# Expert weights in consecutive rows per partition, with features and activations in the matching order

## The chip, the cores and the metric

One core of a Trainium2 chip runs the whole program. The metric is device time in microseconds from the first to the last work of one execution. The engines are named as the profile names them: PE is TensorE (PEld its weight loads), DVE is VectorE, ACT is ScalarE, POOL is GpSimd, and SP is the engine whose queue issues the weight transfers.

## The reference, cut to what matters

Two transformer blocks on 256 tokens of 1024 features, in float32. The first block ends in a mixture of 32 experts, four of them for each token. This is the part that the change touches:

```
def clamped_swiglu(hdn):
    x_glu = jnp.minimum(hdn[..., :D_EXPERT], SWIGLU_LIMIT)
    x_lin = jnp.clip(hdn[..., D_EXPERT:], -SWIGLU_LIMIT, SWIGLU_LIMIT)
    return x_glu * jax.nn.sigmoid(SWIGLU_ALPHA * x_glu) * (x_lin + 1)

def expert_block(args):
    xb, e = args
    hdn = xb @ w_gate_up[e] + b_gate_up[e]          # [rows, 1024] @ [1024, 2048]
    return clamped_swiglu(hdn) @ w_down[e] + b_down[e]   # [rows, 1024] @ [1024, 1024]
```

Both matrix products sum over 1024 rows of a weight matrix. The sum doesn't depend on the order of the rows, as long as the other operand lists its features in the same order.

## The kernel before

**Weights.** Each expert has 12 MB of weights: `w_gate_up` in four chunks of 256 rows, `w_down` in two chunks of 512 rows, 2 MB each. The function `fill` issues them on the SP queue (L208), in the order of `plan`, as soon as a tile of the ring is free; eight tiles of 128 partitions by 16 KB are in use in most of the stage, and a chunk's tile becomes free when `release` is reached after its last product. Before the change, partition p of a `gu` chunk holds rows p and 128 + p of the chunk (two runs of 8 KB), and partition p of a `dn` chunk holds rows p, 128 + p, 256 + p and 384 + p (four runs of 4 KB).

**Features.** `h2t` holds the normed tokens (tokens on partitions, 1024 features along the row). `gain_h2` (L959, POOL) multiplies by the gain, which `along` has spread over all partitions (L805, PE, and L813, ACT), and `h2_rows` (L969, DVE) adds the shift, also spread by `along`. Expert 0's features are gathered from `h2t` at L1068, those of the others by `gather` (L1114).

**One expert.** The loop runs over 32 experts. `gate_up` makes 64 products (L1157, two halves of 64 PE columns side by side) and starts its sums with the bias (L1147). Then DVE and ACT apply the activation: L1162 (minimum, from PSUM), L1164 (sigmoid, ACT), L1165 (product), and then for each half of 256 columns L1168 (clip, from PSUM into `lin`) and L1169 (plus one, times `sig`). PE transposes `lin` in four pieces (L1175), ACT copies the result to `aT` (L1179), and `down` makes 32 products (L1197). Behind each `gate_up` and each `down` stands a branch (L1419, L1462) for experts with more than 64 tokens; three experts take it here (9, 13 and 20, counted from 0), and `act_q` (L1269 to L1274) is the same activation for their further slots.

**Order between experts.** Two experts' outputs are summed into the tokens at once. So an expert with an even number from 4 on begins its activation while PE still has `combine2` (L1220, 16 products) of the pair before to do; an expert with an odd number has only two transposes there (`sgT`, L1127). Experts 0 to 2 also gather the next expert's features at this place (L1114).

Of the kernel before, what the change touches and what calls it, by code (L numbers as in the profile page):

```python
# [27 lines left out]
OP = mybir.AluOpType  # L28
# [11 lines left out]
# columns of the per-partition vectors (vecs)  # L40
# [11 lines left out]
def _consts():  # L52
# [15 lines left out]
    # rows of eight heads: sums' high and low parts and ones, on the queries' side and (negated) on the keys'  # L68
# [27 lines left out]
def build(tc, A, out, dbg=None):  # L96
# [51 lines left out]
    for e in range(NE):  # L148
        for j in range(4):
            add(("gu", e, j), A["w_gate_up"][e, 256 * j:256 * j + 256, :].rearrange("(k p) f -> p k f", p=128))  # L150
        for j in range(2):
            add(("dn", e, j), A["w_down"][e, 512 * j:512 * j + 512, :].rearrange("(k p) f -> p k f", p=128))
# [27 lines left out]
    def fill():  # L180
        while state["issued"] < len(plan):
# [6 lines left out]
            # the slot that has been free for the longest time  # L188
# [11 lines left out]
            if i == last_e + 3:  # L200
                # the last chunks before block 2 come in parts
                for f in (slice(0, 1024), slice(1024, 2048)):
                    nc.sync.dma_start(dst[:, :, f], src[:, :, f])
            elif i in (last_e + 4, last_e + 5):
                for k in (slice(0, 2), slice(2, 3), slice(3, 4)) if i > last_e + 4 else (slice(0, 2), slice(2, 4)):
                    nc.sync.dma_start(dst[:, k], src[:, k])
            elif i >= 6:
                nc.sync.dma_start(dst, src)  # L208
# [13 lines left out]
    def split(pool, src, shape, tag, bufs, pattern=None):  # L222
        """src (float32) = hi + lo, both of 12 significant bits"""
# [6 lines left out]
    class Stream:  # L230
        """pieces of weights, 512 columns each, split ahead of their products"""
# [33 lines left out]
    def cols(key, kk=KD, tiles_=4):  # L265
        """pieces of a column chunk: 128 columns, four rows of k-tiles each"""
# [7 lines left out]
    def krows(key, nk, n=512):  # L274
        """pieces of a chunk: 512 columns of one k-tile"""
        m = n // 512
        return [(key, lambda c, i=i: c[:, 512 * i:512 * i + 512], i == nk * m - 1) for i in range(nk * m)]
# [6 lines left out]
    def rstd_of(pool, ps_sum, n, eps, newton=None):  # L284
        """1/sqrt(ps_sum/n + eps), [128, T]; a step of Newton's where newton gives its scratch"""
# [16 lines left out]
    # ================= block 1: modulation, projections, attention =================  # L302
# [7 lines left out]
    # only for the first eight heads  # L310
# [27 lines left out]
    # the first chunks come in parts, in the order of their use  # L338
# [14 lines left out]
    # at column 5 of a stationary, zeros around it: 32 columns from 5 - r on give row r of the product  # L353
    nc.vector.tensor_copy(cs32[:, :, 5], sg)

    # silu(c) along the rows of all partitions
# [11 lines left out]
    # modulation: mod[n] = sum_d silu(c)[d] W[d, n] + b  # L368
# [3 lines left out]
    # of a chunk's features, DVE sums two tiles (their rows transposed), and PE the other two  # L372
# [9 lines left out]
    def ada_rows(j, r, tag="sc"):  # L382
        """row r of the next sums takes the products with chunk j"""
# [13 lines left out]
    def ada_sum(n, dst, b, row=None, tag="sc", bufs=2):  # L397
        """sums over the four groups of rows, features on partitions: dst and b are [128, 2, n]"""
# [7 lines left out]
    # sum of squares of x  # L406
# [30 lines left out]
    def first_products(n, k):  # L437
        """the four tiles of chunk n of w_in, the products of one k-tile"""
# [51 lines left out]
    def gain(name, sc0, g):  # L490
        """g * (1 + scale)"""
# [4 lines left out]
    # MoBA: the bias of a head is a function of q - k; row p has key k at column 127 - p + k of the table. The table goes  # L496
    # out 16 times, and comes back 16 rows at a time that start one element earlier each
# [21 lines left out]
    # projections  # L519
# [29 lines left out]
    # b_gate_up and b_down as exact sums of three bfloat16 parts  # L549
    bg = keep.tile([128, 3072], BF, name="bg")  # L550

    def expert_bias(i):
        """in three stages, for the columns of different calls"""
# [32 lines left out]
    # forget gates (four times, at rows 0..31): log_sigmoid, running sums  # L586
# [24 lines left out]
    def forget_b():  # L611
        """the sums as two parts of 12 bits each, so that a head's bias is one product of exact terms"""
# [26 lines left out]
    # attention  # L639
# [77 lines left out]
    # the other projections and the rest of the modulation run between the heads  # L717
# [50 lines left out]
    # out projection, tokens on partitions: its products with the heads that are through run between the later heads  # L768
# [4 lines left out]
    def out_products(n):  # L773
        """n of the 32 products, two to a piece of weights"""
# [25 lines left out]
    def along(dst, col, tag="sc", bufs=2, cs=(0, 1)):  # L800
        """a value per feature, along the rows of all partitions"""
        for c in cs:
            p = ps.tile([128, 512], F32, name=tag, bufs=bufs)
            for i in range(4):
                nc.tensor.matmul(p[:, 128 * i:128 * i + 128], lhsT=col[:, 4 * c + i:4 * c + i + 1].to_broadcast(  # L805
                    [128, 128]), rhs=ident, start=True, stop=True, skip_group_check=True)
# [8 lines left out]
    def logits_rows(t, tag, bufs):  # L815
        """what the router makes of xT's tokens t, four groups of rows to be summed"""
# [11 lines left out]
    for h in range(8, 17):  # L828
# [27 lines left out]
        if h == 14:  # L856
            # the part of the router's logits that comes from the shift
# [6 lines left out]
        if h == 15:  # L864
            xt = pa.tile([128, 2, D], F32, name="qkb")
            nc.scalar.dma_start(xt, A["x"])
            # and the part that comes from x before its own norm is known
# [14 lines left out]
    # the products are through: the room of their operands goes to the ring  # L882
# [6 lines left out]
    # the last chunks of the modulation, while the norms and the router wait  # L889
# [19 lines left out]
    def rstd1(dst, tt):  # L909
        """from the two halves' mean squares"""  # L910
# [11 lines left out]
    # post norm and residual, tokens on partitions: x1 = x + rstd * t. The router's logits take t as it is  # L922
# [12 lines left out]
    def turned(tt, src):  # L935
        """features on partitions"""
# [18 lines left out]

    def gain_h2(tt):
        for i in range(4):
            s = slice(256 * i, 256 * i + 256)
            nc.gpsimd.tensor_mul(h2t[:, tt, s], xt[:, tt, s], gfb[i])  # L959
# [31 lines left out]
    along(gfb, gain_["f"])  # L991
# [26 lines left out]
    along(shb, mod[:, 24:32])  # L1018
# [6 lines left out]
    # router  # L1025
# [22 lines left out]
    # slot of a token at an expert; far away where the expert isn't chosen  # L1048
# [15 lines left out]
    # the first expert's slots, at once with features on partitions  # L1064
# [10 lines left out]
    # ================= experts =================  # L1075
# [14 lines left out]
    def slots(e, r, pair=None, S=None):  # L1090
        """one-hot of 64 slots of the expert at its tokens, plain and times the gate: the first 64, or those from
        32 + 64 r on. The gated ones of two experts share a tile, a further round has its own twice"""
# [16 lines left out]
    def gather(S):  # L1109
        """rows of the slots: [(half of the features, slot), 512]"""  # L1110
# [9 lines left out]
    def gatherT(x, r=0):  # L1120
        """k-tile 4 h + c of the slots' features lies at [:, c, 64 h:]"""
# [15 lines left out]
    def gate_up(e, xe, r=0, hook=None):  # L1137
# [3 lines left out]
        for j in range(4):  # L1141
            w = None if r else chunk(("gu", e, j)).rearrange("p (k f) -> p k f", k=2)
            for i, p in enumerate((pg, pl_)):
# [5 lines left out]
                for kk in range(2):  # L1149
                    k = 2 * j + kk  # L1150
                    if r:
                        wk = again(A["w_gate_up"][e, 128 * k:128 * k + 128, 1024 * i:1024 * i + 1024])
# [14 lines left out]
        for c in (slice(0, 256), slice(256, 512)):  # L1167
            nc.vector.tensor_scalar(l[:, c], pl_[:, c], 7.0, -7.0, op0=OP.min, op1=OP.max)  # L1168
            nc.vector.scalar_tensor_tensor(l[:, c], l[:, c], 1.0, s[:, c], op0=OP.add, op1=OP.mult)  # L1169
        return l  # L1170

# [10 lines left out]
    def down(e, at, r=0):  # L1182
# [6 lines left out]
        for c in range(2):  # L1189
            w = None if r else chunk(("dn", e, c)).rearrange("p (k f) -> p k f", k=4)  # L1190
            for j in range(4):
                if r:
                    wk = again(A["w_down"][e, 512 * c + 128 * j:512 * c + 128 * j + 128, :])
# [10 lines left out]
        # two experts' rows on top of each other  # L1204
# [24 lines left out]
    # slots 64 .. 95: 32 slots in each column tile  # L1229
# [37 lines left out]
    def act_q(p, l):  # L1267
# [4 lines left out]
        nc.vector.tensor_scalar(l, p[64:128], 7.0, -7.0, op0=OP.min, op1=OP.max)  # L1272
        nc.vector.scalar_tensor_tensor(l, l, 1.0, g, op0=OP.add, op1=OP.mult)
        nc.vector.tensor_mul(l, l, s)  # L1274
# [25 lines left out]
    # position buckets of block 2 (both signs), then its bias table: a step at each expert  # L1300
# [53 lines left out]
    # pieces of the weights of block 2  # L1354
    def by_half(p):
        """four tiles of two pieces: first all the first halves"""
# [41 lines left out]
    for e in range(NE):  # L1398
        if e == 2:
            # the smallest ring is through: its room goes to what comes later  # L1400
# [3 lines left out]
        if e == NE - 1:  # L1404
            # the last rings are through: their room goes to the pieces of block 2
# [5 lines left out]
        # an expert with more than 64 tokens: 32 further slots  # L1411
# [14 lines left out]
        def hook(j):  # L1426
# [4 lines left out]
            # a chunk of the first experts makes room at once  # L1431
# [39 lines left out]
    # experts with more than 96 tokens: rounds of 64 slots, which load the weights again  # L1471
# [14 lines left out]
    # the last two experts' rows, post norm  # L1486
# [29 lines left out]
    # ================= block 2 =================  # L1516
# [4 lines left out]
    def begin(xh, xl, g, make_x, add, third):  # L1521
        """splits x * g and starts with four tiles of products, with the rest of the norm. make_x(k) completes a
        k-tile of x"""
# [5 lines left out]
        def products(k):  # L1529
# [5 lines left out]
            for t in range(4):  # L1535
                # a bank starts once, and the tile that comes second in it writes on the cleared flags
# [124 lines left out]
    def mixer(make_x):  # L1661
# [12 lines left out]
        # the second ring is through: its two tiles hold what the mixer keeps  # L1674
# [108 lines left out]
        # the attention's steps, then the Fourier branch's, between the tiles of the projections  # L1783
        k_tile2(0)
        # lambda
# [16 lines left out]
        # rstd with tokens on partitions  # L1802
# [60 lines left out]
    def out_proj(k):  # L1863
        # the products are two tiles ahead of the sums, which read banks that no product writes
# [144 lines left out]
```

## Time and profile before

| | us |
|---|---|
| median of 3 runs (1783.46 to 1786.46) | 1783.85 |
| span of the profiled execution | 1783.1 |
| expert stage in it (first L1157 to last L1197) | 214.8 to 1203 |

The profile's busy times are shares of the whole span; the expert stage is 55% of it and has its own limits, so the rows below are mostly of that stage. A timeline row gives the start, the duration, the engine and line, the tile written and the tiles read, the shapes and the count of instructions merged; in brackets stands the idle time of the engine before it and who ended that. The clock column (PEclk) is the granted TensorE clock as a share of 2.4 GHz; the chip grants either 1.2 or 2.4 GHz here, and a window with a value in between holds both.

### The profile page before, as it was taken

How to read it: one execution, taken by the hardware profiler on the slowest of the kernel's cores; microseconds unless marked ns; L12 is line 12 of the kernel's file. 1: busy time of each engine (PE TensorE's matmuls, PEld its weight loads, DVE VectorE, ACT ScalarE, POOL GpSimd, SP SyncE). 2: the span in 40 equal slices, each digit the busy share in tenths (PEclk: the TensorE clock that was granted, in tenths of full speed). 3: DMA queues.
4: the chain of work that ended last, by engine and by line, in shares of the span. 5: the costliest groups of instructions: out<-in, count | busy, mean ns of one | idle time of the engine just before them, and what ended most of it. 6: DMA issues, size and time to landing. Idle time of an engine off the chain costs nothing. (4 is left out here: it accounts for less than half of the span.)

```text
span 1783.1 us, 25545 instructions
## 1 busy us (share of the span) xinstructions
PE 1666.5 (93%) x10162; PEld 1061.4 (60%) x10162; DVE 780.9 (44%) x1627; ACT 525.8 (29%) x1113; POOL 91.3 (5%) x98
## 2 busy tenths in 40 slices
PE   6999999999989989999999999997999999999998
PEld 5787633333433333333333333336999989999997
DVE  5776613232432432324211111115766777676665
ACT  4544310111111011011111101114555555665444
POOL 3501100000000000000000000002000000310000
PEclk8999999999999999999999999998999999999999
DMA  9878799999989988999889999993544453344530
GB/s 353 329 221 332 281 372 410 385 415 418 414 352 380 415 329 361 416 416 415 355 364 415 418 414 417 415 415 145 189 172 184 189 207 142 142 150 182 214 142 25
DMA packets 89005, 548.81 MB, mean 308 GB/s; under 512 B 5064, under 2 KB 7912, under 8 KB 49448
## 3 DMA queue, kind: packets, MB, share of 16 engines
q1 hardware_dynamic: 88424, 544.55, 77.1%
q8 instruction: 115, 1.88, 0.4%
q0 software_dynamic: 272, 0.92, 0.2%
q10 hardware_dynamic: 144, 1.05, 0.2%
q14 instruction: 50, 0.41, 0.1%
HBM read 545.25 MB, written 1.25 MB: 306 GB/s over the span
## 5 line engine op out<-in xcount | busy, mean ns | idle before, releaser
L1157 PE MATMUL h<-ring,xe 128*64 128x512 f32 x2048 | 465.5, 593 | 5.6 <-ACT xe L1080 0.4
L251 DVE TENSOR_TENSOR wl<-ring,wh 128x512 fp32r<-128x512 f32 x421 | 285.1, 710 | 116.3 <-ACT wh L250 109.5
L1157 PEld LDWEIGHTS h<-ring,xe 128*64 128x64 f32 x2048 | 165.6, 136 | 250.5 <-issue 246.5
L250 ACT ACTIVATE wh<-ring 128x512 fp32r<-128x512 f32 x424 | 248.9, 622 | 107.6 <-PE gu L281 85.1
L1197 PE MATMUL h<-ring,aT 128*64 128x512 f32 x1024 | 234.8, 612 | 5.5 <-ACT aT L1179 5.5
L280 PE MATMUL gu<-ring,wh 128*128 128x256 f32 x704 | 201.2, 286 | 2.9 <-ACT ring L1541 2.9
L281 PE MATMUL gu<-ring,wh 128*128 128x256 f32 x704 | 200.4, 285 | 1.9 <-DVE ring L1545 1.9
L282 PE MATMUL gu<-ring,wl 128*128 128x256 f32 x704 | 200.4, 285 | 0.0
L1162 DVE TENSOR_SCALAR glu<-h 128x512 f32<-128x512 f32 x32 | 22.1, 692 | 370.8 <-PE h L1157 370.8
L1197 PEld LDWEIGHTS h<-ring,aT 128*64 128x64 f32 x1024 | 72.6, 141 | 148.7 <-issue 134.4
L1213 DVE COPY y<-h 64x512 f32<-64x512 f32 x32 | 22.2, 694 | 310.2 <-ACTq L1462 285.7
L280 PEld LDWEIGHTS gu<-ring,wh 128*128 128x128 f32 x704 | 135.9, 193 | 3.5 <-ACT ring L1541 3.3
L281 PEld LDWEIGHTS gu<-ring,wh 128*128 128x128 f32 x704 | 135.9, 193 | 2.2 <-DVE ring L1545 2.1
L282 PEld LDWEIGHTS gu<-ring,wl 128*128 128x128 f32 x704 | 135.9, 193 | 0.0
L1117 ACT ACTIVATE glu<-rot 128x512 f32<-128x512 f32 x31 | 18.5, 597 | 276.9 <-PE rot L1114 274.4
L280 PE MATMUL pd<-acth,wh 128*128 128x256 f32 x352 | 98.7, 280 | 0.1
L281 PE MATMUL pd<-actl,wh 128*128 128x256 f32 x352 | 98.3, 279 | 0.1
L282 PE MATMUL pd<-acth,wl 128*128 128x256 f32 x352 | 98.2, 279 | 0.0
L1212 ACT ACTIVATE y<-h 64x512 f32<-64x512 f32 x31 | 18.3, 590 | 220.7 <-PE h L1197 123.1
L1350 DVE COPY_PREDICATED bias<-bm,vecs 128x512 f32<-128x512 uint8 x124 | 80.1, 727 | 1.1
L280 PE MATMUL gu<-big_h,wh 128*128 128x256 f32 x256 | 74.6, 291 | 0.0
L282 PE MATMUL gu<-big_h,wl 128*128 128x256 f32 x256 | 71.5, 279 | 1.1 <-DVE wl L251 1.1
(422 smaller groups left out, 2287.1 us busy)
## 6 DMA issues: line engine op xcount, KB each, us to landing
ring<-in_w_gate_up SPq DMA_DIRECT2D x127, 2048.0 KB, 14.0
ring<-in_w_down SPq DMA_DIRECT2D x62, 2048.0 KB, 19.8
ring<-in_ffn_gu SPq DMA_DIRECT2D x22, 2048.0 KB, 7.8
ring<-in_win SPq DMA_DIRECT2D x12, 2048.0 KB, 8.5
ring<-in_ffn_wd SPq DMA_DIRECT2D x10, 2048.0 KB, 9.5
ring<-in_ada SPq DMA_DIRECT2D x8, 2048.0 KB, 11.1
ring<-in_wout SPq DMA_DIRECT2D x4, 2048.0 KB, 8.1
ring<-in_ada SPq DMA_DIRECT2D x4, 1024.0 KB, 12.6
```

What stands on the lines that cost most here:

```text
L250: nc.scalar.activation(dh, src, AF.Copy)
L251: (eng or nc.vector).tensor_tensor(dl, src, dh.bitcast(F32), op=OP.subtract)
L280: nc.tensor.matmul(o, lhsT=wh, rhs=mh, start=start, stop=False, skip_group_check=True)
L281: nc.tensor.matmul(o, lhsT=wh, rhs=ml, start=False, stop=False, skip_group_check=True)
L282: nc.tensor.matmul(o, lhsT=wl, rhs=mh, start=False, stop=stop, skip_group_check=True)
L1117: nc.scalar.activation(x, p, AF.Copy)
L1157: nc.tensor.matmul(p[64 * hf:64 * hf + 64], lhsT=x, rhs=wk[:, 512 * hf:512 * hf + 512], start=False, stop=(k == KD - 1), skip_group_check= ...
L1162: nc.vector.tensor_scalar(g, pg, 7.0, None, op0=OP.min)
L1197: nc.tensor.matmul(py[64 * oh_:64 * oh_ + 64], lhsT=at[:, j, 64 * c:64 * c + 64], rhs=wk[:, 512 * oh_:512 * oh_ + 512], start=False, stop= ...
L1212: nc.scalar.activation(pair["y"][o:o + 64, 0:512], py[0:64], AF.Copy)
L1213: nc.vector.tensor_copy(pair["y"][o:o + 64, 512:1024], py[64:128])
L1350: nc.vector.copy_predicated(bias2[:, h], m, val[:, :, None].to_broadcast([128, 2, T]))
```

## The change

A chunk is now read as consecutive rows: partition p of a `gu` chunk holds rows 2p and 2p + 1, and partition p of a `dn` chunk rows 4p to 4p + 3, in either case one run of 16 KB. So the tile numbered kk in a `gu` chunk holds the features 2p + kk, and the tile numbered j in a `dn` chunk the activations 4p + j. `h2t` is stored in that order: `along` writes the gain and the shift in the new order (PE writes PSUM in steps of 128 columns, two at a time), and `gain_h2` reads the tokens in natural order and writes them in the new one. The activation reads its PSUM sums and `sig` in steps of four columns (16 bytes) and writes `lin` in consecutive columns, so that the four transposes find their columns next to each other. The number of instructions and their order on every engine are as before; DVE's, POOL's and PE's named instructions have other access patterns. The last three chunks of the last expert still come in parts.

```
-            add(("gu", e, j), A["w_gate_up"][e, 256 * j:256 * j + 256, :].rearrange("(k p) f -> p k f", p=128))
+            add(("gu", e, j), A["w_gate_up"][e, 256 * j:256 * j + 256, :].rearrange("(p k) f -> p k f", p=128))
-            add(("dn", e, j), A["w_down"][e, 512 * j:512 * j + 512, :].rearrange("(k p) f -> p k f", p=128))
+            add(("dn", e, j), A["w_down"][e, 512 * j:512 * j + 512, :].rearrange("(p k) f -> p k f", p=128))
+            elif i >= 6 and key[0] in ("gu", "dn"):
+                nc.sync.dma_start(t[0:parts, 0:cols], src.rearrange("p k f -> p (k f)"))
...
+                o = p[:, 128 * i:128 * i + 128]
+                if sorted_:
+                    o = p[:, 256 * (i // 2):256 * (i // 2) + 256].rearrange("p (k h q) -> p h q k", k=2, h=2)[:, i % 2]
...
-            nc.gpsimd.tensor_mul(h2t[:, tt, s], xt[:, tt, s], gfb[i])
+            nc.gpsimd.tensor_mul(h2t[:, tt, s].rearrange("p (k q) -> p q k", k=2),
+                                 xt[:, tt, s].rearrange("p (q k) -> p q k", k=2),
+                                 gfb[i][:, :].rearrange("p (k q) -> p q k", k=2))
...
-        for c in (slice(0, 256), slice(256, 512)):
-            nc.vector.tensor_scalar(l[:, c], pl_[:, c], 7.0, -7.0, op0=OP.min, op1=OP.max)
-            nc.vector.scalar_tensor_tensor(l[:, c], l[:, c], 1.0, s[:, c], op0=OP.add, op1=OP.mult)
+        for c in (slice(0, 2), slice(2, 4)):
+            lc = l[:, :].rearrange("p (k q) -> p k q", k=4)[:, c]
+            nc.vector.tensor_scalar(lc, fourths(pl_)[:, c], 7.0, -7.0, op0=OP.min, op1=OP.max)
+            nc.vector.scalar_tensor_tensor(lc, lc, 1.0, fourths(s)[:, c], op0=OP.add, op1=OP.mult)
+    def fourths(t):
+        return t[:, :].rearrange("p (q k) -> p k q", k=4)
...
-        nc.vector.tensor_scalar(l, p[64:128], 7.0, -7.0, op0=OP.min, op1=OP.max)
-        nc.vector.scalar_tensor_tensor(l, l, 1.0, g, op0=OP.add, op1=OP.mult)
-        nc.vector.tensor_mul(l, l, s)
+        l = l[:, :].rearrange("p (k q) -> p k q", k=4)
+        nc.vector.tensor_scalar(l, fourths(p[64:128]), 7.0, -7.0, op0=OP.min, op1=OP.max)
+        nc.vector.scalar_tensor_tensor(l, l, 1.0, fourths(g), op0=OP.add, op1=OP.mult)
+        nc.vector.tensor_mul(l, l, fourths(s))
```

## Rows read from the trace of the kernel before

**Rows 1.** The page's first part: busy time, share, instructions of each engine.

```profile
PE 1666.5 (93%) x10162; PEld 1061.4 (60%) x10162; DVE 780.9 (44%) x1627; ACT 525.8 (29%) x1113; POOL 91.3 (5%) x98
```

**Rows 2.** Windows of the expert stage: busy (x count) by engine, clock, DMA share, GB/s.

```profile
460.00:710.00 250.00, 230.22 (x1202) 92.69 (x1202) 83.03 (x173) 30.06 (x68) 0.00 (x0) 0.98 0.92 373
960.00:1210.00 250.00, 225.03 (x1054) 90.24 (x1050) 39.17 (x93) 28.30 (x62) 0.00 (x0) 0.98 1.02 416
```

**Rows 3.** PE's waits in the expert stage: total us, times, longest us.

```profile
PE h L1147 <- ACTq L1462: 21.8, 28, 1.1
PE rot L1175 <- DVEq L1419: 20.1, 14, 1.6
PE rot L1175 <- DVE lq L1272: 2.6, 2, 1.3
```

**Rows 4.** PE's timeline after `gate_up` of an odd and an even expert.

```profile
1020.15 0.41 PE L1127 MATMUL rot<-c,Sg 128*128 128x128 f32 x2 [0.30 <-PEq L1419]
1022.12 0.63 PE L1175 MATMUL rot<-c,lin 128*128 128x128 f32 x4 [1.56 <-DVEq L1419]
...
1048.28 3.69 PE L1220 MATMUL acc<-SgT,y 128*128 128x256 f32 x16
1051.81 0.60 PE L1175 MATMUL rot<-c,lin 128*128 128x128 f32 x4
```

**Rows 5.** DVE's timeline of the same two experts: first and last operation on `lin`.

```profile
1020.24 0.42 DVE L1168 TENSOR_SCALAR lin<-h 128x256 f32<-128x256 f32 x1
...
1021.49 0.42 DVE L1169 SCALAR_TENSOR_TENSOR lin<-lin,sig 128x256 f32<-128x256 f32 x1
...
1049.78 0.42 DVE L1169 SCALAR_TENSOR_TENSOR lin<-lin,sig 128x256 f32<-128x256 f32 x1
```

**Rows 6.** Three lines' instructions: ns of one, minimum/median/maximum, first and last start.

```profile
L1168 DVE TENSOR_SCALAR lin<-h x64: 415/418/421, 231.8 to 1192.8; 128x256 f32<-128x256 f32 x64
L1169 DVE SCALAR_TENSOR_TENSOR lin<-lin,sig x64: 424/425/426, 232.3 to 1193.2; 128x256 f32<-128x256 f32 x64
L959 POOL TENSOR_TENSOR bias<-qkb,mix x8: 721/730/1100, 194.4 to 200.6; 128x256 f32<-128x256 f32 x8
```

**Rows 7.** PE's timeline at the same place in expert 9, which takes the branch.

```profile
504.96 0.63 PE L1175 MATMUL rot<-c,lin 128*128 128x128 f32 x4 [1.32 <-DVE lq L1272]
```

**Rows 8.** PE's timeline at the same place in experts 0 and 31.

```profile
233.70 0.63 PE L1175 MATMUL rot<-c,lin 128*128 128x128 f32 x4 [1.29 <-DVEq L1419]
...
1193.03 0.41 PE L1175 MATMUL rot<-c,lin 128*128 128x128 f32 x2 [1.03 <-DVE lin L1169]
```

**Rows 9.** First bias product of experts 3, 4, 5 and 6 on PE.

```profile
300.72 0.41 PE L1147 MATMUL h<-bg,sel 96*64 96x512 bf16 x2 [0.81 <-ACTq L1462]
...
330.70 0.41 PE L1147 MATMUL h<-bg,sel 96*64 96x512 bf16 x2 [0.73 <-ACTq L1462]
...
360.44 0.41 PE L1147 MATMUL h<-bg,sel 96*64 96x512 bf16 x2 [0.80 <-ACTq L1462]
...
388.73 0.41 PE L1147 MATMUL h<-bg,sel 96*64 96x512 bf16 x2 [0.73 <-ACTq L1462]
```

**Rows 10.** Three windows of 5 us, columns as in rows 2.

```profile
320.00:325.00 5.00, 4.78 (x16) 1.69 (x18) 0.00 (x0) 0.66 (x2) 0.00 (x0) 0.66 1.02 433
...
905.00:910.00 5.00, 5.00 (x19) 1.58 (x19) 0.00 (x0) 0.66 (x2) 0.00 (x0) 0.66 1.01 426
...
1020.00:1025.00 5.00, 3.09 (x16) 1.36 (x18) 1.84 (x5) 1.04 (x3) 0.00 (x0) 1.00 1.02 424
```

**Rows 11.** Timeline before the stage: the second `gain_h2`, the second `h2_rows`.

```profile
198.12 3.15 POOL L959 TENSOR_TENSOR bias<-qkb,mix 128x256 f32<-128x256 f32 x4 [0.69 <-DVE qkb L953]
209.12 1.40 DVE L969 SCALAR_TENSOR_TENSOR bias<-bias,sg,sc 128x512 f32<-128x512 f32 x2
```

**Rows 12.** The page's DMA issues: KB each, median us to landing.

```profile
ring<-in_w_gate_up SPq DMA_DIRECT2D x127, 2048.0 KB, 14.0
...
ring<-in_ffn_gu SPq DMA_DIRECT2D x22, 2048.0 KB, 7.8
```

More of the change, by code (lines that the diff above doesn't have):

```diff
@@ L798, in modulation, with along @@
         gain_["f"] = gf
-    def along(dst, col, tag="sc", bufs=2, cs=(0, 1)):
+    def along(dst, col, tag="sc", bufs=2, cs=(0, 1), sorted_=False):
         for c in cs:
@@ L804, in along @@
             for i in range(4):
-                nc.tensor.matmul(p[:, 128 * i:128 * i + 128], lhsT=col[:, 4 * c + i:4 * c + i + 1].to_broadcast(
-                    [128, 128]), rhs=ident, start=True, stop=True, skip_group_check=True)
+                o = p[:, 128 * i:128 * i + 128]
+                if sorted_:
+                    o = p[:, 256 * (i // 2):256 * (i // 2) + 256].rearrange("p (k h q) -> p h q k", k=2, h=2)[:, i % 2]
+                nc.tensor.matmul(o, lhsT=col[:, 4 * c + i:4 * c + i + 1].to_broadcast([128, 128]), rhs=ident,
+                                 start=True, stop=True, skip_group_check=True)
             if dst[0] is None or c and dst[1] is None:
@@ L990, in build @@
     rstd1(rs1, 1)
-    along(gfb, gain_["f"])
+    along(gfb, gain_["f"], sorted_=True)
     turned(0, h2t)
@@ L1017, in build @@
     shb = [None, None]
-    along(shb, mod[:, 24:32])
+    along(shb, mod[:, 24:32], sorted_=True)
     newton(rs2, 1)
@@ L1151, in gate_up @@
                     if r:
-                        wk = again(A["w_gate_up"][e, 128 * k:128 * k + 128, 1024 * i:1024 * i + 1024])
+                        wk = again(A["w_gate_up"][e, 256 * j:256 * j + 256, 1024 * i:1024 * i + 1024].rearrange(
+                            "(p k) f -> p k f", k=2)[:, kk])
                     else:
@@ L1192, in down @@
                 if r:
-                    wk = again(A["w_down"][e, 512 * c + 128 * j:512 * c + 128 * j + 128, :])
+                    wk = again(A["w_down"][e, 512 * c:512 * c + 512, :].rearrange("(p k) f -> p k f", k=4)[:, j])
                 else:
```

## The prediction

> **What bounds the kernel now.** I read the page's busy shares first, then windows of the expert stage, then the waits inside it, then PE's and DVE's timelines around one such wait. The page shows PE busy for 93% of the span [rows 1], and a reader should not stop there. In the expert stage the transfers look just as full: in its last quarter the DMA engines are busy all the time at 416 GB/s [rows 2], and one could think that the weights set the pace. The earlier window speaks against it: PE is as busy there while the DMA share falls to 0.92 and the rate to 373 GB/s [rows 2], because the ring is full and SP waits for PE to release a tile. The waits decide it: of all that PE waits for in this stage, no row names a transfer. What it waits for is a branch after `down` (21.8 us in 28 waits, untouched by the change) and, second, the end of DVE's activation before the transposes of `lin` (20.1 us in 14 waits, and 2.6 us in 2 more) [rows 3]. So the load is at its limit without being late, and the place to look at is the activation.
>
> **The transfers (removed: short runs).** One run of 16 KB takes the place of two of 8 KB or four of 4 KB. The shape is in the trace: `ffn_gu` chunks are 16 KB per partition, and land 7.8 us after issue in a stage with a short queue, against 14.0 us for the `gu` chunks behind a long one [rows 12]. That says that the new shape is no slower, and not how much faster. I cost it at nothing, because PE's products hide it: no product waits for a landing. It is worth time only if PE becomes faster than the loads, and nothing here makes PE faster.
>
> **The four DVE operations of the activation (made slower, on the path).** After the last product of `gate_up`, DVE works through L1162, L1165 and then L1168, L1169, L1168, L1169 on 256 columns each, and PE transposes `lin` only after the last of them: it ends at 1021.49 + 0.42 = 1021.91, and PE starts at 1022.12, 0.21 us later [rows 4, 5]. In this odd expert PE has only two small transposes to do and stands still for 0.30 + 1.56 = 1.86 us [rows 4]; every further nanosecond of the four operations is added to it. In an even expert the last operation ends at 1049.78 + 0.42 = 1050.20, so `lin` could be used at 1050.41, but `combine2` keeps PE until 1051.81 [rows 4, 5]: 1.40 us of cover, so that a longer activation costs nothing there until it is longer by that.
>
> All four now read one operand in steps of 16 bytes: L1168 its PSUM sums, L1169 `sig` in SBUF. The trace has no DVE operation of any length that reads so, and the price must be bounded. From below it is nothing: 0.42 us as now [rows 6]; I see no reason for a gain, since the columns and bytes are the same. From above I take the slowest float32 operation of the same 128x256 shape that the trace has on any engine, POOL's product at 0.73 us [rows 6], which is 0.31 us more. That is an estimate for another engine, chosen as a bound. Between them I take the middle and a little more, 0.17 us each, since a read that can't use its neighbours should cost a good part of a second pass over the columns and not all of it. Four in a row make 0.68 us per expert (bounds 0 and 1.24).
>
> [...]
>
> Where is it exposed? Odd experts from 3 to 29 without the branch: twelve, 12 x 0.68 = 8.2 us. Expert 0, whose wait is also for DVE (1.29 us), and expert 31 (1.03 us) [rows 8]: 2 x 0.68 = 1.4. Experts 9 and 13 take the branch, and PE waits until L1272, the second operation of `act_q`, is through [rows 7]; L1272 reads 512 columns in the new steps, twice 0.17, so 0.68 + 0.34 = 1.02 each, 2.0 together. Expert 1 and all even experts have cover. Sum of the waits: 8.2 + 1.4 + 2.0 = 11.6 us (bounds 0 and 12 x 1.24 + 2 x 1.24 + 2 x 1.86 = 21.1; the cover of 1.40 us in even experts holds in either case).
>
> **The clock behind a longer gap.** Experts 5 and 3 are the same work, but 5 takes 388.73 - 360.44 = 28.29 us and 3 takes 330.70 - 300.72 = 29.98 us [rows 9]. The 1.69 us between them are the clock: in expert 3 the window after the wait for `lin` shows a granted clock of 0.66, that is, 1.2 GHz for most of it, while expert 25 after the same wait shows 1.00 [rows 10]. Four of the twelve odd experts have such a window, from expert 3 at 320 us to expert 21 at 905 us [rows 10], and the other eight have none, so a gap of 1.86 us stands at the edge. A gap of 2.54 us should be followed by it more often. Bounds: no further drop, or all eight further ones, 8 x 1.69 = 13.5 us. I take the middle, four, 6.8 us.
>
> **Before the stage (POOL, PE).** `gain_h2` writes in steps of 128 columns. Its last piece ends at 198.12 + 3.15 = 201.27, and the first reader that is late on the path is `h2_rows` at 209.12 [rows 11]: 7.85 us of cover for 8 x 0.73 = 5.8 us of POOL work [rows 6], so even a doubling is hidden by DVE's router steps. But POOL and DVE get in each other's way there (a POOL piece takes 0.72 to 1.10 us, [rows 6]), and the sixteen strided PSUM writes of `along` may cost PE something. I take 1 us, with bounds 0 and 5 (the first from no slowing, the second from POOL's second half of 3.15 us and half of that again for DVE).
>
> **Sum.** 11.6 + 6.8 + 1 = 19.4 us. The profiled execution has a span of 1783.1 us, 0.75 below the median of 1783.85; 1783.1 + 19.4 + 0.75 = 1803.3, and I forecast **1803 us**.
>
> **The rivals.**
> - *The strided reads are free.* Then DVE's rows stay at 0.42, the gap and the clock stay, and the hidden transfers change nothing: 1784, with one or two drops of the clock more or less. For it speaks the nearest row, the operation itself at 0.42 [rows 6]. [...]
> - *Only one of the two memories charges.* Then two operations per expert pay: 14 x 0.34 + 2 x 0.34 = 5.4 us of waits if it is SBUF, two more drops of the clock (3.4), 0.5 before the stage: 1793.
> - *The steps cost as much as POOL's operation or more.* 21.1 us of waits, eight drops (13.5), 5 before the stage: 39.6, or 1823.
> - *Faster.* If the four operations cost less than 0.1 us together, the expert stage shifts by the time that changes before it, and the drops of the clock, which stand at an edge, may stay away: the four in odd experts are worth 4 x 1.69 = 6.8 us, 1777. It needs both; faster transfers alone give nothing, as no wait is for them.
>
> **How the numbers follow.** About 0.2% (3.6 us) is what a measurement of this kernel can tell from no change. The forecast, four slowed operations between 1797 and 1815, gets 0.50. One memory alone gets 0.22, free reads 0.12, the dear steps 0.12, faster 0.04. The two slower rivals and the forecast make slower 0.84; free reads make same 0.12. For the range I leave out free reads and faster (0.16) and a small part of the dear case: 1786 to 1823.
>
> **What would show it.** The rows of L1168 and L1169 should read about 0.59 us instead of 0.42; this is the step on which nearly all rests. PE's wait before L1175 in odd experts should be near 2.2 us instead of 1.56, while even experts show no wait there. Of the twelve odd experts about eight should take 1.69 us longer through a window at half clock. PE should still have no wait for a transfer, SP's waits should be longer and the transfer rate in saturated windows at least 416 GB/s. The prediction is wrong if L1168 and L1169 stay at 0.42; if PE turns out to have waited for landings all along, so that the stage becomes shorter with the load; or if the 16 KB runs move below 416 GB/s, so that the last quarter has to wait for them.

## The result and the profile after

The changed kernel takes 1797.67 us (median of 1794.74, 1797.67 and 1800.06) where the kernel before, on the same chip in the same session, takes 1784.27 us. A fourth execution of the changed kernel, of 1832.15 us at a lower granted clock (0.930 against 0.976 to 0.980 in the other three), fell in a slower state of the chip and is left out. The ratio is 1.0072, with a 95% interval of 1.0056 to 1.0088, so the changed kernel is slower by 0.7%, some 13 us. The profiled execution has a span of 1795.9 us against 1783.1, which is 12.8 us more, and the accounts below are made against these two spans.

The lines of the code moved a little: the bias products of L1147 are now L1156, `gate_up` (L1157) is L1167, the operations on `lin` L1168 and L1169 are L1180 and L1181, the transposes L1175 are L1190, and `gain_h2` (L959) is L966. Where a row names DVEq or ACTq, it is the sequencer of that engine, as in the rows of before.

The page first. Its first part and two lines of its other parts, of the changed kernel:

```profile
PE 1672.6 (93%) x10162; PEld 1061.8 (59%) x10162; DVE 795.7 (44%) x1627; ACT 525.5 (29%) x1113; POOL 91.9 (5%) x98
...
DMA packets 48557, 548.81 MB, mean 306 GB/s; under 512 B 5064, under 2 KB 7912, under 8 KB 16936
...
ring<-in_w_gate_up SPq DMA_DIRECT2D x127, 2048.0 KB, 12.7
```

Against [rows 1] the counts are equal, DVE has 14.8 us more work and PE 6.1 us more. The runs are indeed longer: 48557 packets where the page of before has 89005. A `gu` chunk lands 12.7 us after its issue instead of 14.0 [rows 12].

The operations on `lin` and POOL's product before the stage, ns of one as minimum, median and maximum:

```profile
L1180 DVE TENSOR_SCALAR lin<-h x64: 410/417/430, 232.4 to 1207.7; 128x256 f32<-128x256 f32 x64
...
L1181 DVE SCALAR_TENSOR_TENSOR lin<-lin,sig x64: 607/619/649, 232.9 to 1208.2; 128x256 f32<-128x256 f32 x64
...
L966 POOL TENSOR_TENSOR bias<-qkb,mix x8: 800/808/1172, 192.8 to 199.6; 128x256 f32<-128x256 f32 x8
```

This is the reading that settles most. The four operations per expert split in two kinds. L1180, which reads PSUM in steps of 16 bytes, takes 417 ns, as L1168 did (418). L1181, which reads `sig` from SBUF in the same steps, takes 619 ns against 425 [rows 6]: 194 ns more for 256 columns, or 0.76 ns a column. Two such operations stand in each expert's row: 0.39 us.

The two operations of `act_q` that read SBUF in these steps pay as well, one of them a plain product, while its read of PSUM (L1288) takes 692 ns; before, the two took 682 and 685 ns:

```profile
L1289 DVE SCALAR_TENSOR_TENSOR lq<-lq,glu x3: 1077/1086/1097, 510.5 to 870.5; 64x512 f32<-64x512 f32 x3
...
L1290 DVE TENSOR_TENSOR lq<-lq,sig x3: 1075/1096/1102, 511.7 to 871.6; 64x512 f32<-64x512 f32 x3
```

Together these are DVE's 14.8 us: 64 x 0.194 = 12.4 and six times some 0.41, which is 2.4.

PE's waits in the expert stage, total us, times, longest us:

```profile
PE rot L1190 <- DVEq L1435: 25.1, 14, 1.9
PE h L1156 <- ACTq L1478: 21.7, 28, 1.1
...
PE rot L1190 <- DVE lq L1288: 3.4, 2, 1.7
...
PE rot L1190 <- DVE lin L1181: 1.2, 1, 1.2
```

The wait for DVE before the transposes grew from 20.1 to 25.1 us, the one for `act_q` in experts 9 and 13 from 2.6 to 3.4 [rows 3], and the one in expert 31 from 1.03 to 1.2 [rows 8]: 6.0 us in all. The wait after `down` is as it was, and again no wait is for a transfer.

One odd expert without a drop of the clock on PE (expert 17), and the same moment on DVE; a row is start, duration, operation, and in brackets the idle time before it:

```profile
754.73 0.41 PE L1156 MATMUL h<-bg,sel 96*64 96x512 bf16 x2 [0.80 <-ACTq L1478]
...
772.07 0.41 PE L1136 MATMUL rot<-c,Sg 128*128 128x128 f32 x2 [0.30 <-PEq L1435]
774.41 0.63 PE L1190 MATMUL rot<-c,lin 128*128 128x128 f32 x4 [1.93 <-DVEq L1435]
...
783.39 0.41 PE L1156 MATMUL h<-bg,sel 96*64 96x512 bf16 x2 [0.73 <-ACTq L1478]
```

```profile
772.16 0.42 DVE L1180 TENSOR_SCALAR lin<-h 128x256 f32<-128x256 f32 x1
772.61 0.62 DVE L1181 SCALAR_TENSOR_TENSOR lin<-lin,sig 128x256 f32<-128x256 f32 x1
773.14 0.42 DVE L1180 TENSOR_SCALAR lin<-h 128x256 f32<-128x256 f32 x1
773.59 0.61 DVE L1181 SCALAR_TENSOR_TENSOR lin<-lin,sig 128x256 f32<-128x256 f32 x1
```

DVE ends at 773.59 + 0.61 = 774.20 and PE starts 0.21 us later, as before. PE's wait is 1.93 us where it was 1.56 [rows 4]: 0.37 more, which is two longer L1181. The expert takes 783.39 - 754.73 = 28.66 us against 28.29 before [rows 9], again 0.37. So in an undisturbed odd expert the whole difference is these two operations.

The rest is the clock. Experts 5 and 6 of the changed kernel, and a window inside expert 5 (columns as in [rows 2]):

```profile
361.96 0.41 PE L1156 MATMUL h<-bg,sel 96*64 96x512 bf16 x2 [0.80 <-ACTq L1478]
362.18 0.62 PE L1167 MATMUL h<-ring,xe 128*64 128x512 f32 x2
...
391.84 0.41 PE L1156 MATMUL h<-bg,sel 96*64 96x512 bf16 x2 [0.73 <-ACTq L1478]
...
421.58 0.41 PE L1156 MATMUL h<-bg,sel 96*64 96x512 bf16 x2 [0.80 <-ACTq L1478]
```

```profile
380.00:385.00 5.00, 3.36 (x12) 1.45 (x14) 1.40 (x3) 0.78 (x3) 0.00 (x0) 0.66 1.00 429
```

Expert 5 takes 391.84 - 361.96 = 29.88 us where it took 28.29, and the granted clock behind its wait is 0.66: half the full clock for most of the window (0.50 in each half microsecond from 381.5 to 384.5 us, 1.00 up to 381.0 and again from 385.0). The trace gives the clock as a share only; gigahertz can be had from it as an estimate: two products of 512 bf16 columns side by side (L1156) take 362.18 - 361.96 = 0.22 us at a share of 1.00, 2.3 columns a nanosecond, which is near the 2.4 GHz named with the rows if a column takes one cycle, and no run shows that it does. Of the twelve plain odd experts ten have such a drop now, against four before [rows 10]; experts 5, 7, 23, 25, 27 and 29 are new. Two drops elsewhere went away, one behind expert 13 and one in expert 31. Even expert 6 takes 421.58 - 391.84 = 29.74 us, the same as an even expert before (expert 4, 360.44 - 330.70, [rows 9]).

The account: 6.0 us of longer waits, 0.4 us by which the expert stage starts later (its first product at 214.47 instead of 214.07), and the remaining 6.4 us, by subtraction, in stretches at the lower clock. That is 12.8. The plain odd experts alone lost more to the clock: their ten drops make them 16.5 us longer than undisturbed ones, against 6.5 for the four before, which is 10.0 more; so what went away elsewhere gave back some 3.6, by subtraction.

### The profile page after: what moved, and what is told of

The parts are those of the page before. It is cut to its first block, busy times and chain, and to the rows that moved or that the text cites. A ratio compares the mean times of both kernels' runs of the same rounds, so it can differ in the third digit from the quotient of the medians.

```text
span 1795.9 us, 25545 instructions
## 1 busy us (share of the span) xinstructions
PE 1672.6 (93%) x10162; PEld 1061.8 (59%) x10162; DVE 795.7 (44%) x1627; ACT 525.5 (29%) x1113; POOL 91.9 (5%) x98
## 2 busy tenths in 40 slices
DMA packets 48557, 548.81 MB, mean 306 GB/s; under 512 B 5064, under 2 KB 7912, under 8 KB 16936
## 5 line engine op out<-in xcount | busy, mean ns | idle before, releaser
L1167 PE MATMUL h<-ring,xe 128*64 128x512 f32 x2048 | 465.6, 594 | 5.6 <-PEq L1435 1.5
L1167 PEld LDWEIGHTS h<-ring,xe 128*64 128x64 f32 x2048 | 165.5, 137 | 250.9 <-issue 245.7
L1212 PE MATMUL h<-ring,aT 128*64 128x512 f32 x1024 | 241.2, 626 | 4.6 <-ACT aT L1194 4.6
L1172 DVE TENSOR_SCALAR glu<-h 128x512 f32<-128x512 f32 x32 | 22.1, 691 | 369.2 <-PE h L1167 369.2
L1228 DVE COPY y<-h 64x512 f32<-64x512 f32 x32 | 22.2, 694 | 311.7 <-ACTq L1478 290.0
L1126 ACT ACTIVATE glu<-rot 128x512 f32<-128x512 f32 x31 | 18.5, 597 | 277.7 <-PE rot L1123 269.0
## 6 DMA issues: line engine op xcount, KB each, us to landing
ring<-in_w_gate_up SPq DMA_DIRECT2D x127, 2048.0 KB, 12.7
ring<-in_ada SPq DMA_DIRECT2D x4, 1024.0 KB, 12.7
```

The costliest lines, as they stand in the source:

```text
L1126: nc.scalar.activation(x, p, AF.Copy)
L1167: nc.tensor.matmul(p[64 * hf:64 * hf + 64], lhsT=x, rhs=wk[:, 512 * hf:512 * hf + 512], start=False, stop=(k == KD - 1), skip_group_check= ...
L1172: nc.vector.tensor_scalar(g, pg, 7.0, None, op0=OP.min)
L1212: nc.tensor.matmul(py[64 * oh_:64 * oh_ + 64], lhsT=at[:, j, 64 * c:64 * c + 64], rhs=wk[:, 512 * oh_:512 * oh_ + 512], start=False, stop= ...
L1228: nc.vector.tensor_copy(pair["y"][o:o + 64, 512:1024], py[64:128])
```

## The experiments

The theory after the result has two steps. First, only the reads from SBUF in steps of 16 bytes cost, and the transfers give nothing back. Second, a longer wait of PE is more often followed by a drop of the clock, so that a wait costs more than its own length. The rivals: the transfers or the new order of `h2t` take part in the loss; the drops come from the other weight traffic and not from the wait.

**Each half alone.** The first kernel is the kernel before with the new activation and the old loads, the second the changed kernel with the old activation.

```
# act_only: before, with
-        for c in (slice(0, 256), slice(256, 512)):
...
+        for c in (slice(0, 2), slice(2, 4)):
+            lc = l[:, :].rearrange("p (k q) -> p k q", k=4)[:, c]
+            nc.vector.tensor_scalar(lc, fourths(pl_)[:, c], 7.0, -7.0, op0=OP.min, op1=OP.max)
+            nc.vector.scalar_tensor_tensor(lc, lc, 1.0, fourths(s)[:, c], op0=OP.add, op1=OP.mult)
# act_q likewise
# loads_only: after, with the same lines the other way round
```

In both, the order of `lin` doesn't match the rows of `w_down`; the number and size of all operations are as they were.

> The kernel before with the strided activation alone (weights, features and gain as before, so that `lin` comes in an order that no longer matches the weights). Theory W, the wait: only the SBUF reads of `sig` in steps of 16 bytes cost; L1169's counterpart takes 0.62 us instead of 0.42, PE's waits for `lin` grow by 0.37 to 0.39 us in 14 experts, the granted clock drops behind more of the odd experts (8 to 11 of 12 instead of 4), and the time is 1793 to 1800 us. Rival L, the loads and the gather: the new runs of the weights or the permuted features cost the time; then this kernel stays at 1784.

> The changed kernel with the activation's reads made consecutive again, so that `lin` no longer matches `w_down`; the 16 KB runs and the permuted features stay. Theory W: the waits are back at 1.56 us in odd experts, about 4 drops of the clock, and 1784 to 1787 us (0.4 us later start of the expert stage, and a drop of the clock more or less). Rival L: 1795 to 1799, as the changed kernel.

The activation alone takes 1795.70 us, a ratio of 1.0072 (1.0054 to 1.0091), the same as the whole change. The loads alone take 1783.81 us, 1.0000 (0.9988 to 1.0012). PE's wait and DVE's group (busy us, mean ns, then the idle time before it), of the activation alone:

```profile
PE rot L1179 <- DVEq L1424: 25.4, 14, 2.1
...
L1170 DVE SCALAR_TENSOR_TENSOR lin<-lin,sig 128x256 f32<-128x256 f32 x64 | 39.6, 619 | 2.2
```

and of the loads alone:

```profile
PE rot L1189 <- DVEq L1433: 20.0, 14, 1.6
...
L1180 DVE SCALAR_TENSOR_TENSOR lin<-lin,sig 128x256 f32<-128x256 f32 x64 | 27.2, 425 | 2.2
```

So the loss belongs to the activation, and the 16 KB runs with the new order of `h2t` are neither a gain nor a loss. In the first kernel 8 of the 12 odd experts have a drop (in its fastest execution, 1791.88 us, which is the one profiled), in the second 3. This clears the transfers of the drops as well.

**The order made in another place.** The whole change, but `sig` is put in the new order when the minimum of `glu` reads PSUM, so that no operation reads SBUF in steps of 16 bytes.

```
# psum_order: after, with
-        nc.vector.tensor_scalar(g, pg, 7.0, None, op0=OP.min)
+        nc.vector.tensor_scalar(g[:, :].rearrange("p (k q) -> p k q", k=4), fourths(pg), 7.0, None, op0=OP.min)
...
-            nc.vector.scalar_tensor_tensor(lc, lc, 1.0, fourths(s)[:, c], op0=OP.add, op1=OP.mult)
+            nc.vector.scalar_tensor_tensor(lc, lc, 1.0, s[:, :].rearrange("p (k q) -> p k q", k=4)[:, c], op0=OP.add,
+                                           op1=OP.mult)
# act_q likewise
```

> The whole change, but the order is made where the activation reads PSUM: the minimum reads its sums in steps of four columns and writes consecutive ones, so that the sigmoid, the product and `sig` are in the new order already, and no operation reads SBUF in steps. Theory W with free PSUM steps: the minimum stays at 0.69 us, the four operations at 0.42, waits of 1.56 us, 1784 to 1787 us. If a PSUM read in steps of 16 bytes costs at 512 columns what the SBUF read costs, the minimum takes 1.08 us and the time stays at 1795 to 1800.

It takes 1783.41 us, 0.9996 (0.9984 to 1.0007): all of the loss is gone, with the long runs kept. Its rows:

```profile
PE rot L1191 <- DVEq L1436: 20.1, 14, 1.6
...
L1172 DVE TENSOR_SCALAR glu<-h 128x512 f32<-128x512 f32 x32 | 22.1, 692 | 370.8 <-PE h L1167 370.8
...
L1181 DVE SCALAR_TENSOR_TENSOR lin<-lin,sig 128x256 f32<-128x256 f32 x64 | 27.2, 425 | 2.2
```

L1172 reads 512 PSUM columns in the new steps here and consecutively in the changed kernel; it takes 692 ns here and 691 there. So the read in steps of 16 bytes is free from PSUM at both lengths (417 ns against 418 at 256 columns), and the loss goes with the read from SBUF. One rival stays open: every operation that reads PSUM in these steps here has one source, and every one that reads SBUF in them has two (`lin` and `sig`, or the pairs of `act_q`). No run separates the memory from the number of sources.

**How short a step is free in SBUF.** The kernel before with both reads of `lin`'s operations in steps of two columns, that is 8 bytes.

```
# step8: before, with
+        for c in range(2):
+            lc = l[:, 256 * c:256 * c + 256]
+            nc.vector.tensor_scalar(lc, pl_[:, :].rearrange("p (q k) -> p k q", k=2)[:, c], 7.0, -7.0, op0=OP.min,
+                                    op1=OP.max)
+            nc.vector.scalar_tensor_tensor(lc, lc, 1.0, s[:, :].rearrange("p (q k) -> p k q", k=2)[:, c], op0=OP.add,
+                                           op1=OP.mult)
```

> The kernel before with both reads of the activation in steps of two columns (8 bytes) instead of four (the order of `lin` then matches no weights). If a step of 8 bytes in SBUF is as dear as one of 16, L1169's counterpart takes 0.62 us and the time is near 1795; if the price is for leaving a 16-byte line at each element, it stays near 0.42 us and the time at 1784. The PSUM read should stay at 0.42 us either way.

```profile
L1171 DVE SCALAR_TENSOR_TENSOR lin<-lin,sig 128x256 f32<-128x256 f32 x64 | 27.2, 425 | 2.2
L1169 DVE TENSOR_SCALAR lin<-h 128x256 f32<-128x256 f32 x64 | 26.7, 417 | 0.0
```

The group of DVE for L1171 reads 425 ns, the price of consecutive columns, and the only execution took 1785.71 us. Here too `lin` and `w_down` don't match. For this operation with two sources, a step of 8 bytes is free and one of 16 costs 194 ns; 12 bytes were not tried.

**A longer wait without any steps.** To see what the wait alone does, the kernel before gets an operation between `sig` and `lin` that multiplies `sig` by one: of 256 columns in the first kernel, two of 512 columns in the second.

```
# long_wait: before, with
         nc.vector.tensor_mul(s, g, s)
+        nc.vector.tensor_scalar(s[:, 0:256], s[:, 0:256], 1.0, None, op0=OP.mult)
# longer_wait: before, with
         nc.vector.tensor_mul(s, g, s)
+        for _ in range(2):
+            nc.vector.tensor_scalar(s, s, 1.0, None, op0=OP.mult)
```

> The kernel before with one more DVE operation between the product and the clip (the first 256 columns of `sig` times 1.0, consecutive). It makes the chain longer by 0.3 to 0.45 us, about as much as the change does, with no strided read. If the length of PE's wait is what brings the clock down, 8 to 11 of 12 odd experts show a drop and the time is 1792 to 1799. If the drops of the changed kernel come from something else (the reads' own load on SBUF, or chance), only the waits grow, 14 x 0.35 us, and the time is 1788 to 1790 with about 4 drops.

> The kernel before with two more DVE operations of 512 consecutive columns between the product and the clip (`sig` times 1.0, twice), so that the chain is longer by some 0.9 us, still less than the 1.40 us of cover in even experts. Waits: 14 x 0.9 = 12.6 us. If a longer wait makes a drop of the clock more certain, 10 to 12 of 12 odd experts show one (6 to 8 more at 1.7 us) and the time is 1806 to 1811. If the drops come at about the same rate whatever the length, the time is 1796 to 1800.

The first takes 1790.70 us, 1.0046 (1.0026 to 1.0067), the second 1806.36 us, 1.0122 (1.0105 to 1.0139). Their waits and added operations, first of the shorter, then of the longer:

```profile
PE rot L1176 <- DVEq L1420: 24.2, 13, 2.0
...
L1166 DVE TENSOR_SCALAR sig<-sig 128x256 f32<-128x256 f32 x32 | 9.4, 294 | 1.1
```

```profile
PE rot L1177 <- DVEq L1421: 32.1, 14, 2.7
...
PE rot L1177 <- DVE lq L1274: 4.5, 2, 2.2
...
L1167 DVE TENSOR_SCALAR sig<-sig 128x512 f32<-128x512 f32 x64 | 27.3, 427 | 2.2
```

An undisturbed odd expert takes 28.61 us in the first (0.32 more than before, where 0.29 was added) and 29.21 in the second (0.92 more). Drops are seen in 6 of the 12 odd experts with 0.32 us more wait, in 8 with 0.92.

The first kernel decides little. 8 to 11 drops and 1792 to 1799 us were expected if the wait is the cause, some 4 drops and 1788 to 1790 us if not; 6 drops and 1790.70 us lie between. Its executions range from 1788.28 to 1795.43 us, and in the profiled one, the fastest, experts 9 and 20 have lost the drop that they have in the kernel before, so that the expert stage as a whole has no more drops than before.

The second kernel says more. It is 22.2 us slower, and PE's waits for DVE are 15.8 us longer by its trace, which leaves some 6 us for the clock, although no read is strided and no load differs. The count missed: ten to twelve of the odd experts were expected, and eight came, no more than the activation alone has with 0.37 us. That the clock pays is better seen in its mean over each whole execution (a share of the full clock): 0.980 to 0.984 in all 35 executions of the kernel before beside these kernels, 0.978 to 0.983 in the six with 0.32 us more wait, 0.978 to 0.980 in the four of the activation alone, 0.977 to 0.979 in the four with 0.92. So longer waits go with a lower clock, but not steadily. A longer wait also moves the moment of every wait behind it, and no run separates the length from the moment.

**The wait filled.** The other way to test the same step: take the wait away. In odd experts the gather of the next expert's features and its transposes are moved from the middle of `gate_up` to behind it, where PE waits for `lin`. No work is left out.

```
# late: in before, after and psum_order
+        late = e < 3 or e % 2 == 1
...
-            if j == 1 and nxt and e > 2:
+            if j == 1 and nxt and not late:
                 ahead["x"] = gather(nxt[0])
-            if j == 2 and nxt and e > 2:
+            if j == 2 and nxt and not late:
...
-        if e < 3:
+        if late and nxt:
             ahead["x"] = gather(nxt[0])
...
-        if e < 3:
+        if late and nxt:
             xe = gatherT(ahead["x"])
```

> The kernel before, but experts with an odd number gather the next expert's features (8 products, 1.9 us of PE) after `gate_up` and not inside it, as experts 0 to 2 do already, so that this work fills PE's wait for `lin`. Theory W: the wait falls from 1.56 us to about 0.4 in twelve experts (14 us), most of the drops of the clock go with it (4 or 5 of 1.7 us), and the time is 1760 to 1768 us. If the transfers are what really holds the stage (rival T), a faster PE only waits for them instead and the time stays above 1778.

> The same move of the gather on the changed kernel as it is, strided `sig` reads and all. Theory W: the gather's 1.9 us now cover the 0.39 us by which the chain is longer, so the cost of the change shrinks from 13 us to 0 to 5: 1760 to 1769. If the strided reads cost in another way than by PE's wait for `lin`, the 13 us stay on top of before_late.

> The same move of the gather on the change with the order made in the PSUM read. Theory W: 1760 to 1768, within 2 us of before_late, since the transfers are early in both. Rival T: the 16 KB runs now decide, and this kernel is faster than before_late by up to 2% of the stage's transfer time (some 5 to 20 us).

On the kernel before this gives 1758.24 us, 0.9863 (0.9844 to 0.9882); on the changed kernel 1762.41 us, 0.9893 (0.9872 to 0.9914); and on the kernel with the order made in PSUM 1754.92 us, 0.9848 (0.9826 to 0.9870), the fastest of all here. The first and the third are faster than the theory had them (1760 us at the least). PE's timeline of an odd expert of the first, and three of its waits:

```profile
1050.98 1.94 PE L1114 MATMUL rot<-bias,S 128*64 128x512 f32 x8 [0.30 <-PEq L1420]
1052.94 0.41 PE L1127 MATMUL rot<-c,Sg 128*128 128x128 f32 x2
1053.66 0.66 PE L1175 MATMUL rot<-c,lin 128*128 128x128 f32 x4 [0.31 <-ACT glu L1117]
...
PE rot L1175 <- ACT glu L1117: 6.0, 15, 1.1
...
PE h L1157 <- DMA ring<-in_w_gate_up: 3.6, 4, 1.3
```

The 1.94 us of gather products (L1114) stand where the wait of 1.56 us was. An odd expert takes 26.75 us instead of 28.29, and the plain odd experts have no drop any more; the mean granted clock of the four executions is 0.987 or 0.988. Twelve times 1.54 us are 18.5, and the four drops were worth 6.5, together 25.0; measured are 1783.75 - 1758.24 = 25.5. That the two are so near is partly luck: experts 9 and 13 are 3.3 us shorter as well, and experts 26, 29 and 30 are 2.6 us longer than undisturbed ones, where PE waits for transfers. The four drops of the kernel before went with this wait.

With the wait filled the change costs less, 1762.41 - 1758.24 = 4.2 us instead of 13, but not nothing. An undisturbed odd expert takes 27.05 us against 26.75, and the changed kernel has a wait that the other has not:

```profile
PE rot L1136 <- DVEq L1436: 5.4, 13, 0.4
...
1057.15 1.94 PE L1123 MATMUL rot<-bias,S 128*64 128x512 f32 x8 [0.30 <-PEq L1436]
1058.68 0.62 DVE L1181 SCALAR_TENSOR_TENSOR lin<-lin,sig 128x256 f32<-128x256 f32 x1
1059.51 0.41 PE L1136 MATMUL rot<-c,Sg 128*128 128x128 f32 x2 [0.42 <-DVEq L1436]
```

The gather ends at 1057.15 + 1.94 = 1059.09 and the longer activation at 1058.68 + 0.62 = 1059.30; PE's two small transposes (`sgT`, L1136) start 0.21 us after it. So the gather doesn't quite cover the activation, and PE waits up to 0.4 us. In the third kernel this wait isn't there.

The first and the third bear on what the long runs are worth. The first is the only one of the three in which PE waits for a transfer in the expert stage: 3.6 us in 4 waits. The third has no such wait. The last quarter of the stage, columns as in [rows 2], first of the short runs, then of the long ones:

```profile
960.00:1180.00 220.00, 202.69 (x954) 80.43 (x950) 34.71 (x82) 24.79 (x56) 0.00 (x0) 1.00 1.02 416
```

```profile
960.00:1180.00 220.00, 201.01 (x947) 84.83 (x946) 34.71 (x82) 24.80 (x56) 0.00 (x0) 0.99 1.01 425
```

With the DMA engines busy all the time in both, the long runs move 425 GB/s and the short ones 416, 2% more. In the same window the changed kernel itself, with its long runs, moves 416 GB/s at a DMA share of 1.00 and a clock of 0.96. The difference of the two kernels, 1758.24 - 1754.92 = 3.3 us, is about the 3.6 us of waits, but that it comes from them is not shown: the intervals of the two ratios overlap, two of the third kernel's four executions take 1757 us, and the two traces also differ in drops of the clock (experts 9 and 20 have one in the first, expert 13 in the third). The expectations were within 2 us if the transfers are early in both, 5 to 20 if they hold the stage; neither came.

## Why the prediction was right, step by step

The forecast was 1803 us and slower; measured are 1798, inside the range. The place was right, and the sum was half again too large: 19.4 us against 12.8. Its first term, the waits, was twice too large, because the step on which nearly all was said to rest held for one of the two lines only. The rival that charges only SBUF, 1793 us, has this right and lies as near to the result as the forecast (4.7 us below, 5.6 above); the range was wide enough for both.

- **Which operations pay: wrong.** The sum took all four operations on `lin` to pay 0.17 us each, 0.68 together. Two pay, the ones that read SBUF, 0.194 each, and an undisturbed odd expert is 0.37 us longer. The waits are 6.0 us longer instead of 11.6. The price of one was near, which is luck: it was the author's estimate, a little above the middle between nothing and the product of another engine, and no run shows 0.17. The number of them was the mistake, and it was the rival "only one of the two memories charges" that had this right. That rival's 5.4 us of waits are close to 6.0; it took two further drops (3.4 us), where the clock took 6.4. PE's wait in an odd expert became 1.93 us, not 2.2.
- **Where it is exposed: right but for one expert.** Odd experts, 0 and 31 wait longer; even experts take 29.74 us as before, since `combine2` covers the 0.39 us; experts 9 and 13 wait 0.8 us more together, where 2.0 were forecast, for the same reason as above: the operation of `act_q` that PE waits for reads PSUM. Expert 1 was said to have cover, but takes 27.73 us instead of 27.49.
- **The clock: right in kind, near in size partly by luck.** Four further drops of 1.69 us made 6.8. The trace shows six further ones in plain odd experts, which cost 10.0 us more, and two fewer elsewhere, which gave back some 3.6: 6.4 by subtraction. The longer of the two added waits and the filled wait support the cause: the first brings the mean clock down without any strided read (0.977 to 0.979 against 0.980 to 0.984), the second takes the drops in the twelve away. The reading of the edge was less sharp than it looked: with nothing changed at this wait 3 or 4 of 12 experts have a drop, with 0.32 us more 6, with 0.37 us 8 or 10, with 0.92 us 8, each counted in one execution. What decides in the single expert stays open.
- **Before the stage: small, its size not shown.** The stage starts 0.4 us later in the profiled pair, where 1 us was forecast, but its start moves by more than that between executions: 212.89 to 214.71 us in the six traces that have the old order before the stage, 214.18 to 217.09 in the five with the new one. POOL's product takes 808 ns instead of 730 (median). That POOL and DVE slow each other there is in the trace of before: DVE's operations on one column (L918 to L920) take 0.15 and 0.16 us ahead of POOL's product and 0.65 to 0.73 beside it, and the two pieces of the product that begin while DVE is at L953 take 0.99 and 1.10 us, the other six 0.72 to 0.73.
- **The transfers: right.** No wait for one in either kernel, and the loads alone give 1.0000. What the prediction named as the condition under which they are worth something, a faster PE, came true with the filled wait: there the short runs make PE wait 3.6 us and the long ones don't.

## What to carry to other kernels

When an order of columns has to be changed, do it in the first read from PSUM, where steps of 16 bytes cost DVE nothing here, and not in a later operation that reads SBUF, where they cost 0.76 ns a column. A wait of the engine that bounds was worth more than its length here, since the clock dropped behind it (18.5 us of waits and 6.5 of drops): before lengthening or accepting one, look for work of the same engine that can be moved into it. A better transfer that no one waits for gave nothing here (a ratio of 1.0000); measure it again when the compute is faster.

## What the runs showed of the hardware

- On DVE, an operation with two sources, one of them single float32 words in SBUF in steps of 8 bytes, takes 425 ns for 256 columns, as with consecutive words, and 619 ns in steps of 16 bytes. An operation whose one source is in PSUM takes 417 ns in steps of 16 bytes, as with consecutive words (418). At 512 columns the steps of 16 bytes take 1086 against 682 ns from SBUF (64 partitions, two sources) and 692 against 691 from PSUM (one source).
- From 960 to 1180 us, with the DMA engines busy (a share of 1.00 to 1.02), runs of 4 and 8 KB moved 416 GB/s (before, and with the wait filled), runs of 16 KB 425 in four kernels (the loads alone, the order made in PSUM, and the two with the wait filled) and 416 in the changed kernel, at a clock of 0.96.
- PE's granted clock fell to 0.50 of the full one behind waits for DVE of 1.6 to 2.7 us: in 3 or 4 of 12 plain odd experts with 1.56 us of wait, 8 or 10 with 0.37 us more, 8 with 0.92 us more, and none with the wait filled.
